# Moving a zero fill from the first mixer to its merge, and four kinds of weight splits from GpSimd to VectorE

## The chip, the cores and the metric

The kernel runs on one core of a Trainium2 chip. The metric is the device time of one execution in microseconds. Engines are named as in the profile: PE (TensorE), DVE (VectorE), ACT (ScalarE), POOL (GpSimd) and SP (SyncE, which here only starts transfers). POOL and ACT start transfers too, each on a queue of its own.

## What is computed

Two layers over 512 tokens of 1024 channels, float32. Each layer has three token mixers on one input, merged by gates, and then a mixture of experts:

```python
def hybrid_mixer(x, w_in, ..., w_up_a, w_up_b, w_up_c, w_out):
    h = x @ w_in                                     # 1024 -> 5632
    u_a, q_b, k_b, v_b, q_c, k_c, v_c, g_c, gate_a, gate_b, gate_c = jnp.split(h, cuts, axis=-1)
    y_a = s5_mixer(u_a, ...)                         # diagonal state space model
    y_b = stick_breaking_attention(q_b, k_b, v_b)
    y_c = chunkwise_retention(q_c, k_c, v_c, g_c, gn_g)
    merged = (jax.nn.sigmoid(gate_a) * (y_a @ w_up_a)
              + jax.nn.sigmoid(gate_b) * (y_b @ w_up_b)
              + jax.nn.sigmoid(gate_c) * (y_c @ w_up_c))
    return merged @ w_out
# then per layer: h = norm(x * ALPHA + mixer(x)); out = norm(h * ALPHA + top-2 of 16 experts(h))
```

## The kernel before

**Products.** Every large product is made of three matmuls of split numbers (`mm3`, L341): a weight `raw` is cast to a high part `wh` on ACT (L337), and the low part `wl = raw - wh` is a subtraction of 128x1024 (L338) on VectorE or on POOL. TensorE then runs high x high (L343), and the two mixed products (L344, L345). `wh` and `wl` have four buffers each in the pool `split`, that is two chunks of two halves.

**Chunks of `w_in`.** Each layer's `w_in` comes in 22 chunks of 256 columns (1 MB), on SP's queue, into two `raw` buffers. Chunk 0 is the S5 input, 1, 2 and 3 are queries, keys and values of the stick-breaking attention, 4 to 9 belong to the retention, and 10 to 21 are the gates, which the merge works off four per branch. Chunks 0, 1, 2 run as `pjf`, chunk 3 as `pjt`. The string `LEND` (L43) says for each chunk which engine makes the low part of each of its halves: 0 is VectorE, 1 is POOL; its last entry holds for all later chunks. A `raw` buffer can be loaded again when both `wl` of the chunk in it are done.

**The attention.** `stick` (L784) runs chunks 1 to 3, then for each unit of heads a score matmul `z`, two sigmoids on ACT (`keep`, `take`, L815 and L816; a table load of ACT goes ahead of the first), a scan and a product on VectorE (L821, L823) and the transposition `pw` on PE (L826).

**S5's power table.** POOL makes parameters of S5 (L578 to L582) and then, in `s5_tables`, the powers `er`, `ei` with help of `Et` in six steps of doubling width, six instructions each (L618 to L623). S5 uses them only after the attention.

**The zero fill.** The experts write into a DRAM tensor `yd` of which 14 blocks of 96 rows by 1024 (the spill rows) must hold zeros. In layer 0, between S5's input and the attention, POOL sets a tile `zr` to zero (L415) and starts two transfers on its own queue (L418), each of 96x14x512 numbers.

**The merge.** For each of 12 gate chunks it loads a piece of an up-projection (`rawu`, cast to `wuh`), runs 48 `pjf` matmuls for the gates and 12 or 24 `up` matmuls. `row_loads` (L955) is a generator: the merge takes one step of it after each chunk, and so spreads the loads of the rows for the later norm (POOL's queue, then POOL's multiplications and additions with `lngb`) over its chunks. `out_proj` follows, with `w_out` loads on SP's queue of which one buffer of each pair lies in the pool `mr`.

**Order.** A scheduler orders the instructions of each engine by priorities when the program is built; each engine then runs its own in that order. `tc.issue_after(x)` keeps what is made under it behind the instruction x. `self.cut` holds the cast and the subtraction of the split that was made last.

Of the kernel before, what the change touches and what calls it, by code (L numbers as in the profile page):

```python
# [9 lines left out]
F32 = mybir.dt.float32  # L10
# [9 lines left out]
P = 128  # L20
T = 512
NT = T // P
D = 1024
# [5 lines left out]
NG = NE - 2  # L29
CAP = 96  # L30
BLOCKS = -(-T // CAP)
SPILL = 2 * T // (CAP + 1) + BLOCKS - 2
# [7 lines left out]
PK = 1  # L40
WGATE = -4
WARM = 16
LEND = ("11", "11", "01", "11", "11", "11", "11", "11", "00")  # L43
BANKS = dict(pj=2, b=2, o=1, z=3)
IN_W = 5632
CHUNK = 8
# [73 lines left out]
class Kernel:  # L120
# [229 lines left out]
    def chunk(self, l, i):  # L350
        if i < len(self.units):
            units, self.units[i] = self.units[i], None
            if units:
                return units
        v, self.early = self.early, None
        if v is None:
            v = self.load_chunk(l, i)
        eng = [self.nc.vector, self.nc.gpsimd]
        hold, self.hold = self.hold, None
        with self.tc.issue_after(hold) if hold else ExitStack():  # L360
            return [self.split_half(v[:, 4 * s:4 * s + 4, :], (4, 256), eng[int(LEND[min(i, len(LEND) - 1)][s])])
                    for s in range(2)]

    def proj_fm(self, l, i, hh):
# [35 lines left out]
    def mixer(self, l, hh, right):  # L400
        with ExitStack() as ms:
            ys = self.slots_of(ms.enter_context(self.pool("ys")), "ys", 8)
            with ExitStack() as rs:
                ev = self.slots_of(rs.enter_context(self.pool("re", "right")), "re", 8)
                with self.pool("s5") as sp:
                    self.mp = sp
                    self.t2 = self.slots_of(sp, "s5", 12)
                    us = self.s5_in(l, hh)
                    self.ahead = AHEAD
                    with self.pool("at", "right") as ap:  # L410
                        self.mp = ap
                        self.t2 = self.slots_of(ap, "at", 14)
                        if l == 0:
                            zr = ys("zr")
                            self.nc.gpsimd.memset(zr, 0.0)  # L415
                            spill = self.y_dram[NG * CAP:, :].rearrange("(i p) d -> p i d", p=CAP)
                            for h in range(2):
                                self.nc.gpsimd.dma_start(spill[:, :, h * T:(h + 1) * T],  # L418
                                                         zr[0:CAP, None, :].to_broadcast([CAP, SPILL, T]))
                        yb = self.stick(l, hh, ys)  # L420
                    self.mp = sp
                    self.t2 = self.slots_of(sp, "s5", 12)
                    ya = self.s5(us, ys)
                rg = ms.enter_context(self.pool("rg"))
                rt = rs.enter_context(self.pool("rt", "right"))
                self.mp = rt
                self.t2 = self.slots_of(rt, "rt", 14)
                yc = self.retention(l, hh, ev, self.slots_of(rg, "yc", 8))
            self.rows = right.enter_context(self.pool("rows", "right"))
            self.mr = right.enter_context(self.pool("mr", "right"))  # L430
            self.t2 = self.slots_of(rg, "mg", 10)
            return self.merge(l, hh, ya, yb, yc)
# [169 lines left out]
    def s5_tables(self):  # L602
        nc = self.nc
        V, G = nc.vector, nc.gpsimd
        w = self.s5w
        En, L, bb, cx = w["En"], w["L"], w["bb"], w["cx"]
        e8 = lambda x: x.rearrange("p (i k) -> p i k", i=8)
        er, ei = e8(self.t2("er")), e8(self.t2("ei"))
        G.memset(er[:, :, 0:1], 1.0)
        G.memset(ei[:, :, 0:1], 0.0)  # L610
        for j in range(6):
            n = 2 ** j
            cr = En[:, 0, :, j:j + 1].to_broadcast([P, 8, n])
            ci = En[:, 1, :, j:j + 1].to_broadcast([P, 8, n])
            a0, b0, a1, b1 = er[:, :, 0:n], ei[:, :, 0:n], er[:, :, n:2 * n], ei[:, :, n:2 * n]
            t01 = self.t2("Et")
            t0, t1 = (e8(t01[:, x * 256:x * 256 + 8 * n]) for x in range(2))
            G.tensor_tensor(a1, a0, cr, OP.mult)  # L618
            G.tensor_tensor(t0, b0, ci, OP.mult)
            G.tensor_tensor(b1, b0, cr, OP.mult)  # L620
            G.tensor_tensor(t1, a0, ci, OP.mult)
            G.tensor_tensor(a1, a1, t0, OP.subtract)
            G.tensor_tensor(b1, b1, t1, OP.add)  # L623
        into = [[], []]
        for h in range(2):
            hs = slice(4 * h, 4 * h + 4)
            f = [4, CHUNK - 1, 16]
            b = [bb[:, r, hs, None, :].to_broadcast([P, *f]) for r in range(2)]
            lam = [L[:, r, hs, 0:CHUNK - 1][:, :, ::-1][:, :, :, None].to_broadcast([P, *f]) for r in range(2)]
            for r in range(2):  # L630
                full = self.t2("vb")
                v = full.rearrange("p (i j c) -> p i j c", i=4, j=CHUNK)
                o = v[:, :, 0:CHUNK - 1]
                x = self.t2("vx")[:, 0:4 * (CHUNK - 1) * 16].rearrange("p (i j c) -> p i j c", i=4, j=CHUNK - 1)
                V.tensor_tensor(o, b[0], lam[r], OP.mult)
                V.tensor_tensor(x, b[1], lam[1 - r], OP.mult)
                V.tensor_tensor(o, o, x, (OP.subtract, OP.add)[r])
                nc.scalar.copy(v[:, :, CHUNK - 1], bb[:, r, hs])
                ps = self.bank("b", "vT")
                for i in range(4):  # L640
                    nc.tensor.transpose(ps[:, i * P:(i + 1) * P], full[:, i * P:(i + 1) * P], self.ident)
                vt = self.t2("V")
                nc.scalar.copy(vt, ps)
                into[r].append(vt)
        tt = self.mp.tile([P, 16 * P], F32, tag="T", name="T", bufs=1)
        t4 = tt.rearrange("p (i g x) -> p i g x", i=8, g=2)
        G.memset(tt, 0.0)
        dI = self.t2("dI")[0:16, 0:256].rearrange("p (i g c) -> p i g c", i=8, g=2)
        d = self.part(w["sm"], "s5_d")[0:16].rearrange("p (i g) -> p i g", g=2)
        V.tensor_tensor(dI, self.ident[0:16, None, None, 0:16].to_broadcast([16, 8, 2, 16]),  # L650
                        d[:, :, :, None].to_broadcast([16, 8, 2, 16]), OP.mult)
        for g in range(2):
            gs = slice(g * 64, g * 64 + 64)
            for h in range(2):
                ps = self.bank("b", "lag")[0:16]
                for i in range(4):
                    for r in range(2):
                        nc.tensor.matmul(ps[:, i * P:(i + 1) * P], bb[gs, r, 4 * h + i],
                                         cx[r][gs, 4 * h + i, 0:CHUNK].rearrange("p m c -> p (m c)"),
                                         start=r == 0, stop=r == 1, skip_group_check=True)  # L660
                hs = slice(4 * h, 4 * h + 4)
                p3 = ps.rearrange("p (i x) -> p i x", i=4)
                nc.scalar.copy(t4[0:16, hs, g, 16:], p3[:, :, 16:])
                V.tensor_tensor(t4[0:16, hs, g, 0:16], p3[:, :, 0:16], dI[:, hs, g], OP.add)
        for j in range(1, CHUNK):
            t3 = tt.rearrange("p (g x) -> p g x", g=16)
            nc.sync.dma_start(t3[j * 16:(j + 1) * 16, :, j * 16:], t3[0:16, :, 0:(CHUNK - j) * 16])
        return er, ei, into, tt
# [286 lines left out]
    def row_loads(self, l):  # L955
        nc = self.nc
# [15 lines left out]
        V.tensor_reduce(self.rc, ps[:, 0:2 * KD * NE].rearrange("p (x k e) -> p x e k", x=2, k=KD), AX.X, OP.add)  # L972
        V.tensor_tensor(self.rc[:, 1], self.rc[:, 1], self.rb, OP.add)
        gb = self.ln_load((self.mr, 2), *(("ln2", l - 1) if l else ("ln0", 0)))
        yield
        for c in range(NT):
            nc.gpsimd.dma_start(self.rt[c], self.h_dram[l][c * P:(c + 1) * P, :])
# [3 lines left out]
                    nc.gpsimd.tensor_tensor(self.rt[c][:, sl], self.rt[c][:, sl], gb[x][:, sl], op)  # L981
            yield
        self.gb = self.ln_load((self.rows, 3), "ln1", l)
        yield

    def out_proj(self, l, mg):
# [581 lines left out]
```

## Time and profile before

| | |
|---|---|
| time, median of 3 runs | 2254.54 us (2254.14 to 2255.88) |
| time of the profiled execution | 2254.74 us |
| its span in the profile | 2253.0 us |
| granted PE clock, mean over the span | 0.977 |
| busy: PE / PE weight load / VectorE | 96% / 72% / 68% |
| busy: ACT / POOL | 55% / 21% |

The span is the time from the first to the last instruction in the trace; the run's own time has 1.74 us around it. Times in the trace are microseconds from the span's start. Layer 0's mixer lies at the start of the span, layer 1's begins at about 1145.

### The profile page before, as it was taken

What the parts mean: (1) busy time and instruction counts of PE and PEld (TensorE: products, weight loads), DVE (VectorE), ACT (ScalarE), POOL (GpSimd) and SP (SyncE); (2) the same over time, 40 slices, a digit from 0 to 9 for tenths busy, and PEclk for the clock granted to TensorE, in tenths of its full rate; (3) what the DMA queues carried; (4) which work ended last, traced back from release to release, by engine and by line L of the source; (5) the groups of instructions that cost most, each with busy time, mean ns of one, the idle gap of its engine ahead of it and who ended that gap; (6) DMA issues with size and microseconds to landing.
All of it is one profiled execution on the core that took longest, in us unless ns stands there. A gap on an engine that the chain in (4) does not pass through costs nothing. (4 is left out here: it accounts for less than half of the span.)

```text
span 2253.0 us, 28020 instructions
## 1 busy us (share of the span) xinstructions
PE 2163.2 (96%) x10500; PEld 1620.2 (72%) x10501; DVE 1540.8 (68%) x1970; ACT 1247.2 (55%) x1580; POOL 479.9 (21%) x509
## 2 busy tenths in 40 slices
PE   7699999999999999999989999999899999999997
PEld 5469678887777777776667887888777777777765
DVE  7144543458988998887853535434799888888877
ACT  3253123336777777776744331233477777777764
POOL 6512051121039930000261302411300000000003
PEclk9799999999999999999999999999999999999999
DMA  5512245327989999997921313352389999999865
GB/s 185 154 29 70 66 150 178 107 94 250 350 297 360 334 361 350 338 366 282 368 94 57 74 56 122 103 187 94 131 310 358 351 356 352 356 351 358 335 258 206
DMA packets 187979, 517.96 MB, mean 230 GB/s; under 512 B 17776, under 2 KB 71664, under 8 KB 187824
## 3 DMA queue, kind: packets, MB, share of 16 engines
q1 hardware_dynamic: 173312, 476.69, 59.1%
q10 hardware_dynamic: 9392, 20.16, 2.6%
q0 software_dynamic: 5120, 19.14, 2.4%
q8 instruction: 85, 1.39, 0.3%
q14 instruction: 70, 0.57, 0.1%
HBM read 490.13 MB, written 22.81 MB: 228 GB/s over the span
## 5 line engine op out<-in xcount | busy, mean ns | idle before, releaser
L338 DVE TENSOR_TENSOR wl<-raw,wh 128x1024 fp32r<-128x1024 f32 x834 | 1018.1, 1240 | 300.9 <-ACT wh L337 286.8
L337 ACT CAST wh<-raw 128x1024 fp32r<-128x1024 f32 x872 | 907.5, 1051 | 463.4 <-PE e L345 196.9
L344 PE MATMUL e<-wl,hx 128*96 128x512 f32 x1024 | 407.2, 398 | 7.1 <-PEq L1453 6.3
L345 PE MATMUL e<-wh,hx 128*96 128x512 f32 x1024 | 404.5, 395 | 0.0
L343 PE MATMUL e<-wh,hx 128*96 128x512 f32 x1024 | 391.3, 394 | 0.3 <-ACT wh L337 0.3
L345 PE MATMUL pjf<-hx,wl 128*128 128x512 f32 x608 | 245.6, 404 | 7.3 <-POOL wl L338 7.3
L343 PE MATMUL pjf<-hx,wh 128*128 128x512 f32 x608 | 246.0, 405 | 4.2 <-DVE v L210 4.2
L344 PE MATMUL pjf<-hx,wh 128*128 128x512 f32 x608 | 245.5, 404 | 0.3 <-DVE hx L211 0.2
L344 PEld LDWEIGHTS e<-wl,hx 128*96 128x96 f32 x1024 | 165.7, 162 | 75.5 <-DVEq L1453 7.2
L1421 POOL DMA_INDIRECT yg<-yd,pos x16 | 28.1, 1753 | 882.2 <-DVE wl L338 585.9
L343 PEld LDWEIGHTS e<-wh,hx 128*96 128x96 f32 x1024 | 165.3, 162 | 67.5 <-ACT wh L337 0.9
L345 PEld LDWEIGHTS e<-wh,hx 128*96 128x96 f32 x1024 | 166.4, 162 | 65.8 <-issue 0.5
L344 PE MATMUL e<-wl,gh 128*96 128x512 f32 x512 | 201.3, 393 | 0.2
L345 PE MATMUL e<-wh,gl 128*96 128x512 f32 x512 | 201.4, 393 | 0.0
L343 PE MATMUL e<-wh,gh 128*96 128x512 f32 x512 | 195.0, 394 | 0.0
L345 PEld LDWEIGHTS pjf<-hx,wl 128*128 128x128 f32 x608 | 116.0, 191 | 35.2 <-POOL wl L338 7.7
L343 PEld LDWEIGHTS pjf<-hx,wh 128*128 128x128 f32 x608 | 116.1, 191 | 32.8 <-DVE v L210 5.5
L344 PEld LDWEIGHTS pjf<-hx,wh 128*128 128x128 f32 x608 | 115.9, 191 | 29.1 <-DVE hx L211 1.4
L821 DVE TENSOR_TENSOR_SCAN left<-keep,cs 128x256 f32<-128x256 f32 (+3 forms) x32 | 27.1, 878 | 142.6 <-ACT keep L815 142.6
L338 POOL TENSOR_TENSOR wl<-raw,wh 128x1024 fp32r<-128x1024 f32 x38 | 96.0, 2537 | 91.8 <-ACT wh L337 91.7
L344 PEld LDWEIGHTS e<-wl,gh 128*96 128x96 f32 x512 | 82.7, 162 | 36.3 <-DVE wl L338 2.2
L343 PEld LDWEIGHTS e<-wh,gh 128*96 128x96 f32 x512 | 82.6, 161 | 35.2
(490 smaller groups left out, 2967.2 us busy)
## 6 DMA issues: line engine op xcount, KB each, us to landing
raw<-in_moe_w_dram SPq DMA_DIRECT2D x384, 1024.0 KB, 5.7
raw<-in_w_in_dram SPq DMA_DIRECT2D x44, 1024.0 KB, 5.2
yd<-y ACTq DMA_DIRECT2D x28, 384.0 KB, 4.8
raw<-in_w_out_dram SPq DMA_DIRECT2D x8, 1024.0 KB, 7.4
yd<-zr POOLq DMA_DIRECT2D x2, 2688.0 KB, 22.2
row<-hd POOLq DMA_DIRECT2D x8, 512.0 KB, 7.3
rawu<-in_w_up_c_dram SPq DMA_DIRECT2D x8, 512.0 KB, 3.5
tab<-in_ct_dram ACTq DMA_DIRECT2D x12, 256.0 KB, 2.8
```

Source lines behind the costliest of these rows:

```text
L337: self.cut = (nc.scalar.copy(hv, v).ins, (eng or nc.vector).tensor_tensor(lv, v, hv.bitcast(F32), OP.subtract).ins)
L338: (eng or nc.vector).tensor_tensor(lv, v, hv.bitcast(F32), OP.subtract).ins)
L343: mm(out, lh, rh, start=start, stop=False)
L344: mm(out, lh, rl, start=False, stop=False)
L345: mm(out, ll, rh, start=False, stop=stop)
L821: V.tensor_tensor_scan(lf[:, 0:n][:, ::-1], keep[:, at:at + n][:, ::-1], self.zero.to_broadcast([P, n]), 1.0, OP.mult, OP.add)
L1421: nc.gpsimd.indirect_dma_start(out=yg[j], out_offset=None, in_=Y[:, :], in_offset=bass.IndirectOffsetOnAxis(ap=r["pos"][:, j, c:c + 1], ax ...
```

## The change

Three edits. The zero fill leaves the place ahead of the attention; in layer 0 `row_loads` now makes a zero tile of 96x1024 in the pool `mr` and starts 14 transfers of 384 KB on ACT's queue, three per step of the generator. `LEND` becomes a table for each layer. And each step of the power table is kept behind `self.cut[1]`.

```diff
-LEND = ("11", "11", "01", "11", "11", "11", "11", "11", "00")
+LEND = (("11", "11", "00", "00", "01", "01", "01", "01", "00"), ("11", "00", "00", "00", "01", "01", "01", "01", "00"))
...
-            return [self.split_half(v[:, 4 * s:4 * s + 4, :], (4, 256), eng[int(LEND[min(i, len(LEND) - 1)][s])])
+            return [self.split_half(v[:, 4 * s:4 * s + 4, :], (4, 256), eng[int(LEND[l][min(i, len(LEND[l]) - 1)][s])])
...
-                        if l == 0:
-                            zr = ys("zr")
-                            self.nc.gpsimd.memset(zr, 0.0)
-                            spill = self.y_dram[NG * CAP:, :].rearrange("(i p) d -> p i d", p=CAP)
-                            for h in range(2):
-                                self.nc.gpsimd.dma_start(spill[:, :, h * T:(h + 1) * T],
-                                                         zr[0:CAP, None, :].to_broadcast([CAP, SPILL, T]))
...
             t01 = self.t2("Et")
+            after = ExitStack()
+            after.enter_context(self.tc.issue_after(self.cut[1]))
             t0, t1 = (e8(t01[:, x * 256:x * 256 + 8 * n]) for x in range(2))
...
             G.tensor_tensor(b1, b1, t1, OP.add)
+            after.close()
...
         gb = self.ln_load((self.mr, 2), *(("ln2", l - 1) if l else ("ln0", 0)))
+        if l == 0:
+            zr = self.mr.tile([P, 2048], F32, tag="raw", name="zr", bufs=2)[0:CAP, 0:D]
+            nc.gpsimd.memset(zr, 0.0)
         yield
...
         self.gb = self.ln_load((self.rows, 3), "ln1", l)
+        yield
+        for i in range(SPILL if l == 0 else 0):
+            nc.scalar.dma_start(self.y_dram[(NG + i) * CAP:(NG + i + 1) * CAP, :], zr)
+            if i % 3 == 2:
+                yield
         yield
```

What this does to the order of the engines, first on POOL in layer 0, where S5's parameters (`s5c`) end and the power table stands. `wl_598` and `wl_602` are the low parts of chunk 3, `wl_1423` is of chunk 4. Before:

```order
L582 TENSOR_SCALAR s5c_97<-s5c_97 128x8x16
L415 MEMSET zr_471 128x512
L338 TENSOR_TENSOR wl_598<-raw_595,wh_597 128x1024 [waits DMAHW3_49,PE_49,Activation_49]
L418 DMA yd_74<-zr_471 96x14x512 [waits Pool_49]
L338 TENSOR_TENSOR wl_602<-raw_595,wh_601 128x1024 [waits PE_49,Activation_49]
L418 DMA yd_74<-zr_471 96x14x512
L622 TENSOR_TENSOR er_982<-er_982,Et_993 128x8x2
L623 TENSOR_TENSOR ei_983<-ei_983,Et_993 128x8x2
L338 TENSOR_TENSOR wl_1423<-raw_1420,wh_1422 128x1024 [waits DMAHW4_49,PE_49,Activation_49]
```

And now, from the same parameter row; the rest of the table stands between, and then the two low parts that POOL keeps here, the second halves of chunks 4 and 5:

```order
L575 TENSOR_SCALAR s5c_97<-s5c_97 128x8x16
L617 TENSOR_TENSOR er_978<-er_978,Et_989 128x8x2 [waits Pool_49]
L618 TENSOR_TENSOR ei_979<-ei_979,Et_989 128x8x2 [waits Pool_49]
...
L617 TENSOR_TENSOR er_978<-er_978,Et_1017 128x8x32 [waits Pool_49]
L618 TENSOR_TENSOR ei_979<-ei_979,Et_1017 128x8x32 [waits Pool_49]
L338 TENSOR_TENSOR wl_1423<-raw_1416,wh_1422 128x1024 [waits DMAHW4_49,PE_49,Activation_49]
L338 TENSOR_TENSOR wl_1503<-raw_1496,wh_1502 128x1024 [waits DMAHW5_49,PE_49,Activation_49]
```

The memset, chunk 3's low parts and the two transfers are gone from this place.

On VectorE in layer 0 the first scan of the attention (`left<-keep`) stood directly behind S5's parameters (`small`). Now these stand there, `wl_594` and `wl_598` being chunk 3's, `wl_1419` and `wl_1499` the first halves of chunks 4 and 5, `vb` and `vx` S5's tables:

```order
L560 TENSOR_TENSOR small_96<-r_364,q_365 128x128
L338 TENSOR_TENSOR wl_594<-raw_591,wh_593 128x1024 [waits DMAHW3_49,PE_49,Activation_49]
L631 TENSOR_TENSOR vb_1024<-small_96,s5c_97 128x4x112 [waits DVE_49]
L338 TENSOR_TENSOR wl_598<-raw_591,wh_597 128x1024 [waits PE_49,Activation_49]
L632 TENSOR_TENSOR vx_1025<-small_96,s5c_97 128x448 [waits DVE_49]
L633 TENSOR_TENSOR vb_1024<-vb_1024,vx_1025 128x4x112 [waits DVE_49]
L338 TENSOR_TENSOR wl_1419<-raw_1416,wh_1418 128x1024 [waits DMAHW4_49,PE_49,Activation_49]
L338 TENSOR_TENSOR wl_1499<-raw_1496,wh_1498 128x1024 [waits DMAHW5_49,Activation_49]
L817 SCALAR_TENSOR_TENSOR left_712<-keep_708,cs_92 128x256 [waits DMAHW1_49,Activation_49]
```

Four subtractions of weights, and the first tables, have come ahead of the scan. In layer 1 both halves of chunk 1 likewise stand right behind the last `hx` of VectorE, then both of chunk 2.

On ACT in layer 0's merge the transfers of the fill (L985) stand between the casts of chunks 12 to 15 (`wh_2374` is chunk 12's second, `wh_2461` and `wh_2465` are chunk 13's) and the gates' activations (`gsg`):

```order
L337 CAST wh_2374<-raw_2368 128x1024 [waits PE_49]
L985 DMA yd_74<-zr_2249 96x1024 [waits Pool_49]
L930 CAST wuh_2433<-rawu_2366 128x512 [waits DMAHW2_49,PE_49]
L939 ACTIVATE gsg_2363<-pjf_2312 128x512 [waits PE_49]
L263 DMA lngb_2703<-in_ln1_g_dram 128x1024 [waits DMAHW1_49]
L263 DMA lngb_2703<-in_ln1_b_dram 128x1024 [waits DMAHW3_49]
L985 DMA yd_74<-zr_2249 96x1024
L985 DMA yd_74<-zr_2249 96x1024 [waits DMAHW5_49]
L337 CAST wh_2461<-raw_2459 128x1024 [waits DMAHW2_49,PE_49]
L939 ACTIVATE gsg_2444<-pjf_2378 128x512 [waits PE_49]
L985 DMA yd_74<-zr_2249 96x1024 [waits DMAHW6_49]
L337 CAST wh_2465<-raw_2459 128x1024 [waits PE_49,Activation_49]
```

Three pieces stand ahead of chunk 13's casts, and one between them; six follow up to chunk 14's first cast, four more up to the last, ahead of chunk 15's. On SP the order is the same as before; there the second `w_out` load of layer 0 now waits for the last piece, since it goes into the buffer of the zeros.

## Rows read from the trace of the kernel before

**Rows 1.** The page, busy time by engine.

```profile
PE 2163.2 (96%) x10500; PEld 1620.2 (72%) x10501; DVE 1540.8 (68%) x1970; ACT 1247.2 (55%) x1580; POOL 479.9 (21%) x509
```

**Rows 2.** Waits of PE: tile, line, releaser; us in total, times, longest.

```profile
PE pw L826 <- DVE take L823: 22.3, 10, 18.5
...
PE pjf L345 <- POOL wl L338: 7.3, 1, 7.3
...
PE pjt L344 <- POOL wl L338: 3.2, 2, 2.4
```

**Rows 3.** Timeline of VectorE: start, us, line, operation, count; idle before and releaser.

```profile
96.95 1.35 DVE L821 TENSOR_TENSOR_SCAN left<-keep,cs 128x256 f32<-128x256 f32 x2 [47.07 <-ACT keep L815]
```

**Rows 4.** Timeline of ACT in layer 0.

```profile
49.05 1.05 ACT L337 CAST wh<-raw 128x1024 fp32r<-128x1024 f32 x1 [1.77 <-PE pjf L344]
...
92.54 1.04 ACT L337 CAST wh<-raw 128x1024 fp32r<-128x1024 f32 x1 [19.39 <-DMA raw<-in_w_in_dram]
...
96.33 0.60 ACT L815 ACTIVATE keep<-z 128x512 f32<-128x512 f32 x1
```

**Rows 5.** Timeline of POOL in layer 0.

```profile
60.60 2.33 POOL L338 TENSOR_TENSOR wl<-raw,wh 128x1024 fp32r<-128x1024 f32 x1
62.89 1.20 POOL L418 DMA_DIRECT2D yd<-zr  x1
64.11 2.37 POOL L338 TENSOR_TENSOR wl<-raw,wh 128x1024 fp32r<-128x1024 f32 x1
```

**Rows 6.** The page, DMA issues: KB each, median us to landing.

```profile
yd<-zr POOLq DMA_DIRECT2D x2, 2688.0 KB, 22.2
```

**Rows 7.** DMA queues from 25 to 110: packets, MB, share of 16 engines.

```profile
q1 hardware_dynamic: 6205, 6.94, 24.5%
q0 software_dynamic: 1376, 5.51, 22.1%
```

**Rows 8.** Timeline of PE: chunk 3, `pw` and the block of 96, both layers.

```profile
60.27 0.28 PE L343 MATMUL pjt<-wh,hx 128*128 128x256 f32 x1
...
100.77 0.69 PE L826 MATMUL pw<-cs,take 128*128 128x128 f32 x2 [18.53 <-DVE take L823]
...
217.66 0.40 PE L343 MATMUL pjf<-hx,wh 128*128 128x512 f32 x1
...
1191.28 0.28 PE L343 MATMUL pjt<-wh,hx 128*128 128x256 f32 x1
...
1208.94 0.44 PE L826 MATMUL pw<-cs,take 128*128 128x128 f32 x2 [0.69 <-DVE take L823]
...
1321.21 0.40 PE L343 MATMUL pjf<-hx,wh 128*128 128x512 f32 x1
```

**Rows 9.** Timeline of POOL in layer 1.

```profile
1147.83 0.47 POOL L618 TENSOR_TENSOR er<-er,s5c 128x8 f32<-128x8 f32 x1
...
1164.01 4.66 POOL L338 TENSOR_TENSOR wl<-raw,wh 128x1024 fp32r<-128x1024 f32 x2
```

**Rows 10.** Window: busy time of PE, PEld, DVE, ACT, POOL; PE clock, DMA share, GB/s.

```profile
1166.00:1172.00 6.00, 5.60 (x13) 4.44 (x14) 0.00 (x0) 0.00 (x0) 5.13 (x7) 0.50 0.38 111
```

**Rows 11.** Timeline of VectorE in layer 1.

```profile
1155.05 1.63 DVE L211 TENSOR_TENSOR hx<-v,hx 128x512 fp32r<-128x512 f32 x2
1156.60 0.84 DVE L635 TENSOR_TENSOR vb<-small,s5c 128x448 f32<-128x448 f32 x1
1157.36 1.43 DVE L338 TENSOR_TENSOR wl<-raw,wh 128x1024 fp32r<-128x1024 f32 x1
```

**Rows 12.** Windows in layer 0's merge, columns as in rows 10.

```profile
290.00:300.00 10.00, 10.00 (x45) 8.11 (x45) 3.81 (x6) 2.17 (x3) 4.89 (x6) 1.00 1.00 358
300.00:310.00 10.00, 10.00 (x44) 8.09 (x43) 3.90 (x2) 3.60 (x5) 10.00 (x8) 1.00 0.35 118
```

**Rows 13.** Timeline of ACT in the merge, chunk 13's first cast.

```profile
305.01 1.05 ACT L337 CAST wh<-raw 128x1024 fp32r<-128x1024 f32 x1 [9.94 <-DMA raw<-in_w_in_dram]
```

**Rows 14.** Timeline of PE in the merge, chunk 13's first matmul.

```profile
310.72 0.40 PE L343 MATMUL pjf<-hx,wh 128*128 128x512 f32 x1
```

**Rows 15.** Timeline of SP's queue in the merge.

```profile
365.79 1.12 SPq L323 DMA_DIRECT2D raw<-in_w_out_dram  x2
```

## The prediction

> **What bounds the kernel now.** I read the page first: TensorE is busy for 2163.2 of the 2253.0 us of the span [rows 1], so an edit to VectorE, GpSimd (POOL) or the DMA queues is worth only what it takes out of TensorE's idle time, or out of its stretches at the lower clock, which count as busy. So the second view is the list of what TensorE waited for [rows 2]: `pw` behind VectorE's `take` with one wait of 18.5 us, the `pjf` matmul of L345 behind a `wl` on POOL with one wait of 7.3, and the `pjt` matmul of L344 behind a `wl` on POOL, 3.2 in two waits. All three lie where the change works.
>
> The long wait is followed back engine by engine. `pw` needs `take`, and VectorE, idle for 47.07 us, did the scan at 96.95 as soon as `keep` was there [rows 3]. ACT made `keep` only at 96.33, since chunk 5's casts stand ahead of it in its queue, and the first had stood for 19.39 us on the load of chunk 5, which landed at about 92.5 [rows 4]. That load goes into the buffer that chunk 3 leaves, free when POOL has done chunk 3's second `wl`, at 64.11 + 2.37 = 66.5. The zero fill had been started on POOL's queue at 62.89, between the two halves [rows 5], and its two DMAs of 2688 KB took 22.2 us to land [rows 6]. So a 1 MB load took 26 us, about as long as the fill. The view of DMA queues for this stretch says why it lost out: POOL's queue (q0) moved 5.51 MB in 1376 packets, 4.0 KB each, the queue of the loads (q1) 6.94 MB in 6205, 1.1 KB each [rows 7].
>
> Two faults in layer 0, then: chunk 3's `wl` are late (casts done by 50.1 [rows 4], subtractions at 60.60 and 64.11 behind S5's parameters and the memset [rows 5]), and chunk 5's load fights the fill. Layer 1 has no fill, and a short form of the first fault: POOL is in the power table from 1147.83, and does chunk 1's two `wl` only from 1164.01 [rows 9]; after the stall TensorE runs at clock 0.50, the lower of its two levels [rows 10].
>
> **Layer 0, step by step.** Removed from here: one memset and two DMA issues on POOL, 5.5 MB of writes. Moved from POOL to VectorE: the `wl` of both halves of chunk 3, of the first halves of chunks 4 to 7, and of the second half of chunk 2. This last one adds one instruction ahead of chunk 3's. VectorE is idle from 96.95 - 47.07 = 49.9 [rows 3], its S5 parameters behind it, and chunk 3's halves stand next in its row; they are cast by 50.1. A `wl` beside a busy POOL took 1.43 us in layer 1 [rows 11]; with chunk 2's ahead and one `vb` of 0.84 [rows 11] between them both are done by 49.9 + 3 x 1.43 + 0.84 = 55.0. TensorE comes to chunk 3 at 60.27 [rows 8]; the two `pjt` waits are gone, and chunk 5's load can start at about 55 and meet no fill, and its cast waits for nothing but the split buffers, which chunk 3's matmuls give back. That is how layer 1 runs this same stretch, so I use layer 1 as the template: from the first `pjt` of chunk 3 to the first matmul of the next 96-matmul block (`sg`) it takes 1321.21 - 1191.28 = 129.93 us, in layer 0 217.66 - 60.27 = 157.39 [rows 8]. The difference, **27.5**, holds the 18.5 wait, the 3.2, and the stretches at lower clock about them.
>
> Two things make layer 0 a little worse than its template. In the template `pw` starts 1208.94 - 1191.28 = 17.7 us into the stretch, 0.69 of them a wait [rows 8]; by the new order TensorE has fewer chunk 4 matmuls ahead of layer 0's `pw` (eight, and the `vT` transposes), which I estimate to leave 1.8 us idle, 1.1 more. And a gap of that size may drop the clock: the one drop for which I have a price is layer 1's, 13 matmuls in 5.60 us at 0.50 [rows 10], where full clock takes 10.00/44 = 0.23 each [rows 12], so 13 x (0.43 - 0.23) = 2.6; at even odds 1.3. From below the two cost 0, from above 3.7. Layer 0: 27.5 - 1.1 - 1.3 = **25.1** (23.8 to 28, the top for a `pjt` that also starts at full clock).
>
> **Layer 1.** Chunk 1's halves go to VectorE, right behind the last `hx`, whose pair ends at 1155.05 + 1.63 = 1156.7 [rows 11]; the first is done at 1156.7 + 1.43 = 1158.1. TensorE asks for it 7.3 us [rows 2] before POOL's 1164.01 + 2.33 [rows 9], at 1159.1. So the wait of 7.25 goes, and with it the 2.6 of lower clock: 9.8, of which I take **9.7**. Margin on the first half is 1.0 us, and the second half is asked for twelve matmuls (2.8 us) later. Beside the table the two could take twice that, 2.9 each; then the first is 0.5 late and the second 0.6, and a clock drop of 2.6 could come on top: 6.5 at the worst, 10 at best. `vb`, `vx` and the rest now lie behind these; VectorE's next scan comes only before `pw` at 1208.94 [rows 8]. What is late next would be the table on POOL; nothing but chunk 4 and 5's second halves stands behind it.
>
> **The table's edge.** `issue_after(self.cut[1])` names the `wl` instruction made last, which is on VectorE after the edit, while all of the table is on POOL. The orders show the table directly behind S5's parameters, both before and now. I cost it at nothing; its cover is that POOL has no other `wl` here but chunk 4's and 5's second halves. In layer 0 the table can go on where POOL now does the memset and the first `wl`, by 60.60 [rows 5], and the whole of it took 1164.01 - 1147.83 = 16.2 in layer 1 [rows 9], so chunk 4's half is done by 60.6 + 16.2 + 2.4 = 79.2 at the latest; TensorE needs it at its thirteenth matmul of the chunk, four behind `pw`, whose start the template puts at 60.27 + 17.7 = 77.9, with z and `pw` work between: about 80.
>
> **The merge.** Added: 14 DMAs of 384 KB on ACT's queue among gate chunks 12 to 14, one memset of 96x1024 on POOL among the row loads. TensorE is busy in 10.00 of 10 here [rows 12], so only a late cast hurts. The trace has no write of this size issued by ACT here; SP's issues of loads took 1.12/2 = 0.56 us [rows 15], POOL's of the fill 1.20 [rows 5]. So 14 issues are 8 to 17 us, spread over about 30, in which ACT is busy for 2.17 to 3.60 of each 10 [rows 12] and has 20 free: both ends hide, and I take 0. The DMA engines are full from 290 to 300 (share 1.00, 358 GB/s) and at 0.35 in the next ten [rows 12]. The first three pieces fall into the full slice: 1.18 MB at 358 GB/s is 3.3 us, at the 250 GB/s (6.5 MB in 26 us) of the old clash 4.7. Chunk 13's load, which now ends at 305.0 [rows 13], would then give its cast at 308.3 to 309.7; TensorE asks for that chunk at 310.72 [rows 14], but the cast (1.05) and a `wl` (2 beside POOL's row additions, an estimate) have to lie before its third matmul at 311.2. So 308.3 + 3.05 = 311.4 costs 0.2, and 309.7 costs 1.6. I take **0.8**; from below 0. The other eleven pieces meet a DMA that is two thirds idle.
>
> **Sum.** 25.1 + 9.7 - 0.8 = 34.0 off the profiled execution's own 2254.74 us (the span and 1.74 around it) gives 2220.7. The median of the runs is 0.2 lower: **2220.5**.
>
> **Rivals.** (A) The sum above: 0.62.
>
> (B) The fill takes its clash along, 0.18. It is 5.5 MB still, and 5.5/0.358 = 15.4 us of all DMA engines. If pieces pass ahead of the loads as they did in layer 0, chunks 13 and 14 each lose the bytes queued ahead of them: six pieces (2.4 MB, 6.6 us) for chunk 14, or a piece that waits on an earlier DMA holds ACT's queue with casts and `gsg` behind it. Against it: 0.35 share in 300:310 [rows 12], 5.7 us of slack on chunk 13 [rows 13, 14]. Price 3 to 7 more: 2223.5 to 2227.5. The Trainium skill bears on it ("DMA: Bandwidth & Descriptors", Queues, rings and completion order): each DMA engine goes round its queues packet by packet. By that rule a fill in 4 KB packets gets some four fifths from a load in 1.1 KB packets whichever queue it is on, and moving it from POOL's queue to ACT's helps nothing in itself. The trace agrees in layer 0, where the load took 26 us and the fill 22.2 [rows 6, 7].
>
> (C) Layer 0's wait only moves, 0.10: the scan stands in VectorE's row behind chunk 5's first half, and that behind ACT's cast and the split buffers; or chunk 4's second half comes behind a table that VectorE's work drew out. For it: the margin of about 1 us of chunk 4's half, worked out above. Against it: layer 1 has the casts ahead of `keep` too and waits 0.69 [rows 8]. Price about 5, with a clock drop up to 9: 2225 to 2230.
>
> (D) The change doesn't do what it says in layer 0, 0.05: another load, not the fill, held chunk 5, and only layer 1's 9.7 and the 3.2 of `pjt` come: 2241.6.
>
> (E) Slower, 0.05. The second pair of `w_out` loads goes into the buffer of the zeros, so SP's queue now waits there for the last piece, with `moe_w`, `w_up_c` and `w_in` loads behind it. Before, it passed at 365.79 [rows 15]. It decides from the point where the last piece lands after that and TensorE runs out of chunks, some 15 us later; to lose the 34 and 4.5 more the last piece would have to land after 365.8 + 15 + 38.5 = 419, though the spare DMA time holds all the pieces by about 335. Price: above 2259.
>
> **The numbers.** The likeliest is 2220.5; A alone spans 2216 to 2224. The range of 8 in 10 takes in B and C and the best case (28 + 10 - 0): 2215 to 2231. About 0.2% (4.5 us) is what a measurement of this kernel can tell from no change. Faster: A to D less a little for mishaps together, 0.93; same 0.03; slower 0.04.
>
> **What would show it.** Right: no wait of `pw` over 3 us, no `pjt` or `pjf` behind a POOL `wl`, chunk 5's cast on ACT before 75, `sg` at 190 to 194, the merge busy 10.00 of 10 in each ten. Wrong: a TensorE wait on an ACT `wh` or VectorE `wl` in the merge (B), `pw` after 80 (C), SP standing at `w_out` (E). The prediction fails most likely by the merge, whose DMA room I know only by slices of ten.

## The result

The change is faster, by a third less than forecast: 2232.61 us median of five runs (2226.74 to 2239.43), against 2254.54 (2253.45 to 2258.44); the ratio is 0.9896, with a 95% interval of 0.987 to 0.9921. Forecast were 2220.5 and a range of 2215 to 2231. The five times lie further apart than those of before; that turns out to be part of the answer.

The profiled run took 2232.61 us with a span of 2230.8, 22.2 below that of before. Cut at the marks of [rows 8] and others of their kind (first `pjt` of chunk 3, first matmul of `sg`, first of `out_proj`), the two profiles compare so, in us:

| stretch | before | after | gain | forecast |
|---|---|---|---|---|
| layer 0, chunk 3 to `sg` | 157.4 | 145.0 | 12.4 | 25.1 |
| layer 0, `sg` to `out_proj` (holds the merge) | 230.0 | 232.8 | -2.8 | -0.8 |
| `out_proj` and experts, to layer 1's first chunk | 698.7 | 697.2 | 1.5 | 0 |
| layer 1, first chunk to chunk 3 | 44.9 | 34.7 | 10.3 | 9.7 |
| layer 1, chunk 3 to `sg` | 129.9 | 129.3 | 0.6 | 0 |

Layer 1's opening came as worked out, and the miss is layer 0. First the waits of TensorE in the changed kernel: tile, line, releaser; us in total, times, longest.

```profile
PE pw L822 <- DVE take L819: 7.5, 8, 4.3
...
PE pjf L345 <- DVE wl L338: 2.1, 1, 2.1
```

The waits behind a `wl` on POOL [rows 2] are gone from the list, and 18.5 of `pw` has become 4.3. The marks on TensorE's timeline:

```profile
60.21 0.28 PE L343 MATMUL pjt<-wh,hx 128*128 128x256 f32 x1
...
80.11 1.12 PE L822 MATMUL pw<-cs,take 128*128 128x128 f32 x4 [4.33 <-DVE take L819]
...
205.19 0.40 PE L343 MATMUL pjf<-hx,wh 128*128 128x512 f32 x1
...
438.02 0.39 PE L343 MATMUL opj<-wh,hx 128*128 128x512 f32 x1
...
1169.89 0.28 PE L343 MATMUL pjt<-wh,hx 128*128 128x256 f32 x1
```

`pw` comes at 80.11, where I had 77.9. ACT, which held it up before [rows 4], now has chunk 5's cast and `keep` in good time:

```profile
70.49 1.05 ACT L337 CAST wh<-raw 128x1024 fp32r<-128x1024 f32 x1 [3.73 <-PE pjt L345]
...
74.77 0.60 ACT L811 ACTIVATE keep<-z 128x512 f32<-128x512 f32 x1
```

On VectorE the scan, which stood idle-ready before [rows 3], starts 3.7 us after `keep` started (3.1 after it ended), behind the first half of chunk 5:

```profile
49.04 1.64 DVE L338 TENSOR_TENSOR wl<-raw,wh 128x1024 fp32r<-128x1024 f32 x1
...
51.56 1.64 DVE L338 TENSOR_TENSOR wl<-raw,wh 128x1024 fp32r<-128x1024 f32 x1
...
71.57 6.98 DVE L338 TENSOR_TENSOR wl<-raw,wh 128x1024 fp32r<-128x1024 f32 x1 [11.72 <-ACT wh L337]
78.47 1.26 DVE L817 TENSOR_TENSOR_SCAN left<-keep,cs 128x256 f32<-128x256 f32 x2
```

Chunk 3's halves took 1.64 each where 1.43 was priced, and were done by 53.2, ahead of the 55.0 priced. But the half of chunk 5 took 6.98 us, more than four times that. What POOL did in those 7 us:

```profile
72.09 0.73 POOL L618 TENSOR_TENSOR ei<-ei,Et 128x256 f32<-128x256 f32 x1
72.77 4.70 POOL L338 TENSOR_TENSOR wl<-raw,wh 128x1024 fp32r<-128x1024 f32 x2
```

POOL, with the end of the table and the second halves of chunks 4 and 5 (the two that `LEND` leaves it), ran without a gap until 77.47, each instruction at its usual length; VectorE's ended 1.1 us later.

The rest of layer 0's miss is in the clock. Windows: the three columns at the end are PE clock, DMA share, GB/s.

```profile
75.00:80.00 5.00, 0.78 (x4) 0.29 (x2) 5.00 (x5) 1.48 (x4) 2.47 (x2) 0.91 0.70 218
80.00:85.00 5.00, 4.89 (x15) 2.78 (x16) 2.08 (x5) 0.77 (x2) 0.10 (x1) 0.50 0.60 202
...
115.00:120.00 5.00, 5.00 (x23) 2.95 (x22) 2.16 (x5) 2.12 (x5) 0.13 (x2) 0.50 0.02 3
```

After a slice with 0.78 us of work in 5, TensorE is granted 0.50 (1.2 GHz). It happens a second time from 113 to 127, with no wait of `pw` over 0.8 us ahead of it.

In the merge the one wait, 2.1 us, is chunk 13's. The load was late: the cast came 11.4 us after chunk 12's first gate matmul at 284.71, where before it was 8.3 (296.72 to 305.01 [rows 13]). That still left 2.7 us before TensorE asked. Then it looks much like the first wait: VectorE's two `wl` of that chunk took 5.41 us, the first of them 4.28, while POOL did its row additions. Before, the two took 3.99 beside the same additions.

```profile
296.06 1.05 ACT L337 CAST wh<-raw 128x1024 fp32r<-128x1024 f32 x1 [12.98 <-DMA raw<-in_w_in_dram]
```

```profile
297.14 5.41 DVE L338 TENSOR_TENSOR wl<-raw,wh 128x1024 fp32r<-128x1024 f32 x2 [11.47 <-ACT wh L337]
```

```profile
287.81 12.52 POOL L980 TENSOR_TENSOR row<-row,lngb 128x512 f32<-128x512 f32 x10
```

### The profile page after: what moved, and what is told of

The parts are those of the page before. It is cut to its first block, busy times and chain, and to the rows that moved or that the text cites. A ratio compares the mean times of both kernels' runs of the same rounds, so it can differ in the third digit from the quotient of the medians.

```text
span 2230.8 us, 28031 instructions
## 1 busy us (share of the span) xinstructions
PE 2161.2 (97%) x10498; PEld 1617.5 (73%) x10501; DVE 1554.7 (70%) x1986; ACT 1246.3 (56%) x1580; POOL 437.3 (20%) x491
## 5 line engine op out<-in xcount | busy, mean ns | idle before, releaser
L338 DVE TENSOR_TENSOR wl<-raw,wh 128x1024 fp32r<-128x1024 f32 x850 | 1046.1, 1250 | 342.2 <-ACT wh L337 328.6
L345 PEld LDWEIGHTS e<-wh,gl 128*96 128x96 f32 x512 | 82.5, 161 | 34.3
L1212 PE MATMUL gx<-A,hi 128*128 128x288 f32 (+1 forms) x640 | 97.3, 296 | 0.0
```

The lines of the kernel that those rows point to most:

```text
L338: (eng or nc.vector).tensor_tensor(lv, v, hv.bitcast(F32), OP.subtract).ins)
L345: mm(out, ll, rh, start=False, stop=stop)
L1212: nc.tensor.matmul(ps[s], rows[c][:, k * P:(k + 1) * P], A[:, c].rearrange("p e s -> p (e s)"), start=c == 0, stop=c == NT - 1)
```

## The experiments

Three theories stood after this. **1**: VectorE gets no turn while POOL runs instructions that read SBUF back to back; what POOL kept in layer 0 costs the scan, and then the clock. **2**: the clock falls because this attention is thin in matmuls, whatever VectorE does. **3**: part of the miss comes and goes between executions. And of the change's parts (the fill, the subtractions by `LEND`, and the edge, which keeps the table behind the last split) it was open which does what. "Mark" below is the stretch from chunk 3 to `sg` in layer 0: 157.4 before, 145.0 with the change.

**All of chunks 4 and 5 on VectorE (e1).**

```diff
-LEND = (("11", "11", "00", "00", "01", "01", "01", "01", "00"), (...))
+LEND = (("11", "11", "00", "00", "00", "00", "01", "01", "00"), (...))
```

> The changed kernel, but in layer 0 the second halves of chunks 4 and 5 also go to VectorE, so that POOL has no subtraction of weights near the attention's first scan. Theory 1 (the first half of chunk 5 on VectorE took 6.98 us because POOL's table and its two subtractions ran at the same time, and the scan stood behind it): each wl takes under 2 us, the first wait of pw falls from 4.3 to under 1.5 us, the stretch at the lower clock from 80 to 88 is gone, and the time falls by the wait and that stretch, 3.3 + 3.7 = 7, to about 2226. Theory 2 (the clock falls because this attention has few matmuls in flight, whatever VectorE does): the long wl is gone, but the lower clock stays at two places and the time stays within 3 of 2232.

2220.99 us median of five (2218.03 to 2231.3), ratio 0.9852 (0.9832 to 0.9873). VectorE's timeline, then TensorE's:

```profile
71.56 4.49 DVE L338 TENSOR_TENSOR wl<-raw,wh 128x1024 fp32r<-128x1024 f32 x2 [8.93 <-ACT wh L337]
75.98 1.26 DVE L817 TENSOR_TENSOR_SCAN left<-keep,cs 128x256 f32<-128x256 f32 x2
```

```profile
77.61 0.66 PE L822 MATMUL pw<-cs,take 128*128 128x128 f32 x3 [1.14 <-DVE take L819]
```

Two `wl` now take less than one did, though the first of them, beside the table's last steps, took 3.36, where I had expected under 2. `pw` comes 2.5 us sooner, within my 77.6 to 77.9, and the mark is 133.5, a gain of 23.9 where the prediction had 25.1. The lower clock after it shrank to part of one slice (0.69 from 80 to 85), and the second stretch was not there. In e7 below, whose layer 0 is that of e1, and in e6 this lower clock is gone too, and the mark is 132.1 and 132.2: a gain of 25.3 and 25.2. The wait's share is theory 1's; the time fell further than it said.

**Is it POOL's reading (e5 and e6)?** Both kernels are e1 with work added on POOL directly behind layer 0's table, on a tile that is used up by then:

```diff
+                for _ in range(4):
+                    G.tensor_tensor(t01, t01, t01, OP.add)
```

in e5, and in e6

```diff
+                for _ in range(9):
+                    G.memset(t01, 0.0)
```

> e1_c45_vector with four additions of 128x512 on POOL, directly behind layer 0's power table; nothing reads their result, they stand in for the two subtractions that e1 took away from there, and take about as long, 5 us. Theory 1 (a VectorE instruction with two SBUF inputs gets no turn while POOL runs instructions that read SBUF back to back): VectorE's two wl of chunk 5, 4.49 us together in e1 from 71.56, last until POOL is through at about 78.5 and 2.5 more, the scan starts at about 80.5 instead of 75.98, and the first pw at about 82. Rival (the wl was long because of its own data, chunk 5's load or cast): as in e1, 4.5 us, pw at 77.6.

> As e5_pool_adds, but with nine memsets of 128x512 (0.52 us each, 4.7 in all) in place of the additions: POOL is as busy, but reads no SBUF. Theory 1 as the Trainium skill words it (SBUF: the lock holds against a GpSimd operation that reads SBUF): VectorE's two wl end as in e1 once the table is through, within 4.5 to 5 us, scan at about 76, pw at 77.6. Rival (any POOL instruction keeps VectorE out): as e5, scan at about 80, pw at 82.

With the additions, VectorE and POOL:

```profile
71.79 5.30 DVE L339 TENSOR_TENSOR wl<-raw,wh 128x1024 fp32r<-128x1024 f32 x2 [8.95 <-ACT wh L338]
77.02 2.90 DVE L823 TENSOR_TENSOR_SCAN left<-keep,cs 128x256 f32<-128x256 f32 x2
79.84 1.53 DVE L825 TENSOR_TENSOR take<-take,left 128x256 f32<-128x256 f32 x2
```

```profile
74.11 6.64 POOL L625 TENSOR_TENSOR Et<-Et 128x512 f32<-128x512 f32 x4
```

With the memsets:

```profile
71.56 4.48 DVE L339 TENSOR_TENSOR wl<-raw,wh 128x1024 fp32r<-128x1024 f32 x2 [8.93 <-ACT wh L338]
75.97 1.26 DVE L823 TENSOR_TENSOR_SCAN left<-keep,cs 128x256 f32<-128x256 f32 x2
```

```profile
73.88 5.18 POOL L625 MEMSET Et<- 128x512 f32 x9
```

Nine memsets beside them leave VectorE's instructions as they were in e1 to a hundredth; four additions stretch all of them, and `pw` goes to 81.09. So it is what the additions do and the memsets don't, reading SBUF above all, and not POOL's being busy. But the additions did not shut VectorE out as my numbers said: the two `wl` grew by 0.8, the scans took 2.90 instead of 1.26, the products 1.53 instead of 0.72. Each addition depends on the one ahead, the two `wl` of the change do not; that the gaps between dependent additions let VectorE in is a reading of this, not tested. (The times of these single runs, 2231.6 and 2227.8, hold lower clock elsewhere: from 102 to 116 the one, from 1194 to 1208 the other.)

Nor is it a rule that VectorE is the one kept out, as theory 1 has it. In layer 1 of the changed kernel VectorE's four `wl` of chunks 1 and 2 ran beside the table and took 1.40 each. There it was the table's instructions that grew: this one, of 128x128, took 1.44, where in layer 0 it took 0.45.

```profile
1145.48 5.60 DVE L338 TENSOR_TENSOR wl<-raw,wh 128x1024 fp32r<-128x1024 f32 x4
```

```profile
1147.16 1.44 POOL L617 TENSOR_TENSOR er<-er,Et 128x128 f32<-128x128 f32 x1
```

What decides which of the two engines waits, these runs don't settle.

**The change once more (e9).**

> The changed kernel itself once more, for the five times from 2226.7 to 2239.4. If the stretch at the lower clock from 113 to 128 in its profile comes and goes from one execution to the next (theory 3), the profile shows the same first wait of pw of 4.3 and the same lower clock behind it, but the second stretch may be gone or elsewhere, and then layer 0's mark sg is near 199 and the time near 2226. Rival (the second stretch belongs to this order of instructions): it is there again at 113, sg at 205, time within 2 of 2232.6.

2228.56 us median of six (2224.49 to 2238.19), ratio 0.9895 (0.9878 to 0.9912). The profile has the same 4.4 us wait and the clock drop behind it, and where the second stretch was:

```profile
115.00:120.00 5.00, 5.00 (x30) 2.89 (x28) 2.41 (x6) 2.80 (x7) 0.13 (x2) 1.00 0.00 0
```

Full clock. The mark is 136.4, 8.5 less than in the first profile of the same kernel, and the run took 2224.49. By the starts of ACT's instructions, the same in both, 6.1 of the 8.5 lie between 110 and 128. The rest lies about the first drop, 0.50 from 79 to 89 in the first profile and from 81 to 88 here, and about a third stretch, from 164 to 178 there and from 160 to 170 here. Theory 3 holds for the second stretch, and theory 2 falls as it stands: the same instructions in the same order ran at either level. Whether the drop needs a thin attention stays open.

**The fill elsewhere (e2, the edit in part).** In the attention, where the DMA engines have next to nothing to do from 85 to 130 (a share of 0.02 or less in windows of 5 us):

```diff
+                if self.fill and h2 == 0 and unit[0] in ((1, 0), (1, 3)):
+                    with self.tc.issue_after(last):
+                        h = unit[0][1] // 3
+                        nc.gpsimd.dma_start(self.fill[0][:, :, h * T:(h + 1) * T],
+                                            self.fill[1][0:CAP, None, :].to_broadcast([CAP, SPILL, T]))
```

> The changed kernel, but the fill is issued on POOL's queue as two transfers behind the fourth and fifth unit of layer 0's attention, where no load is under way, instead of 14 pieces on ACT's queue in the merge. Theory 1 (the fill holds up chunk 13's load, and with it one wl beside POOL's row additions): the TensorE wait of 2.1 us in the merge goes, from the gates' first matmul of layer 0 to out_proj it takes 230.0 again instead of 232.8, and the time is about 2.8 lower, 2230. Rival (the merge's wait is one of VectorE and POOL alone): the merge still takes over 232, no gain.

2225.03 us median of five (2223.67 to 2235.29), ratio 0.9859 (0.9844 to 0.9874). No TensorE wait is left in the merge, and from chunk 12's first gate matmul to `out_proj` it takes 150.95 us, as before the change, where the changed kernel takes 153.31. So the fill's price in the merge is 2.4 by these two profiles. It is more in others with the fill there: in e9's the same stretch takes 154.76, 3.8 more than before, as the same wait of 2.1 has a stretch at 0.50 from 293 to 296 behind it; e3, e5, e6 and e7 have 154.8 to 154.9, e1 has 153.3. The mark from `sg` that I had named is no good here: it is 233.5, since the clock was lower from 228 to 235, ahead of the merge.

**The fill where it was (e4, against the changed kernel, in part).**

```diff
+                            for h in range(2):
+                                self.nc.gpsimd.dma_start(spill[:, :, h * T:(h + 1) * T],
+                                                         zr[0:CAP, None, :].to_broadcast([CAP, SPILL, T]))
...
-            nc.scalar.dma_start(self.y_dram[(NG + i) * CAP:(NG + i + 1) * CAP, :], zr)
```

> The fill stays where it was, on POOL's queue ahead of the attention; LEND by layers and the edge as in the change. Theory 1 (the fill's fight with chunk 5's load is the greater part of layer 0's loss): layer 1 gains its 10; in layer 0 chunk 3 runs without a wait, but chunk 5's load meets the fill and pw waits some 8 to 15 us. Time 2236 to 2244. Rival (only the late subtractions matter): within 3 of the changed kernel, 2230 to 2236.

2225.77 us median of four (2223.9 to 2227.37), ratio 0.9868 (0.9853 to 0.9883). Both my theories are wrong here. POOL started the fill at 63.17, and ACT's timeline has chunk 5's cast at the same moment as the changed kernel, waiting for TensorE and for no load:

```profile
70.49 1.05 ACT L337 CAST wh<-raw 128x1024 fp32r<-128x1024 f32 x1 [3.73 <-PE pjt L345]
```

With chunk 3's `wl` done at 52.3, its `raw` buffer is free some ten us ahead of the fill, and no clash with that load is left to avoid. `pw` waits 6.0, but for VectorE, whose `wl` beside POOL took 8.44, and the mark is 138.7, 2.3 more than e9's. From `sg` to `out_proj` it takes 230.1 again.

**Fill moved, subtractions left on POOL (e3).** `LEND` as before, the edge kept:

> The fill moved and the table kept behind the last split, with LEND as before in both layers, so all subtractions of chunks 3 to 5 are on POOL. Theory 1 (without the fill, chunk 5's load is in time, and the rest is what VectorE gives): layer 0 keeps part of the gain, chunk 3's low parts come about 0.5 us earlier than before and cost about 2.5 us, and the table runs ahead of chunk 4's, which are then 4 us late; layer 1 gains less than 1, or loses, as its table now stands behind chunk 3. Time 2240 to 2247. Rival (all of layer 0's gain comes from VectorE): over 2250.

2247.58 us median of ten (2236.95 to 2253.56), ratio 0.9965 (0.9953 to 0.9977). Without chunk 3 on VectorE the move of the fill seems to count: the mark is 144.4 in its profile (13.0 less than before). But that profile is of the fastest of the ten, 10.6 below their median, and against the edge alone (e11, below), which differs by nothing but the fill, the intervals of the two ratios just overlap. POOL's four `wl` now hold up the scan itself, on VectorE's timeline:

```profile
78.93 7.01 DVE L817 TENSOR_TENSOR_SCAN left<-keep,cs 128x256 f32<-128x256 f32 x2 [25.70 <-ACT keep L811]
```

**The edge alone (e11)**, in the kernel before:

> The kernel before with nothing but the edge: the table is kept behind the last split, all fill and LEND as before. Theory 1: layer 1's table goes behind chunk 3's subtractions, so the wait of 7.25 there goes without any work for VectorE, 7 to 9 us; in layer 0 the fill still holds chunk 5's load (pw waits some 18), so 2246 to 2249. Rival (the edge does nothing of itself, as I costed it): within 2 of before.

2251.11 us median of ten (2248.19 to 2261.52), ratio 0.9986 (0.9972 to 1.0). That can hardly be told from no change. In the profile layer 1's opening falls from 44.9 to 39.2 us, and its 7.25 wait is gone with no work for VectorE; layer 0's mark is 3.4 longer in its profile, with a wait of 18.0 and lower clock in most slices from 80 to 120.

**Layer 1's splits as before (e7)**, on top of e1:

> e1_c45_vector with layer 1's splits as they were before the change (layer 0 as in e1). My term for layer 1 says 9.7: the wait of pjf behind POOL is back at about 7.2 us, with a stretch at the lower clock, and the time is 9.7 above e1, 2230 to 2231. Rival (layer 1's gain is taken back by its own later waits): within 4 of e1.

2231.77 us median of four (2225.77 to 2233.41), ratio 0.9879 (0.9861 to 0.9898). I had overlooked that the edge stays in force here. POOL's timeline has the table behind chunk 3's halves, no longer ahead of chunk 1's [rows 9]:

```profile
1154.88 0.23 POOL L613 TENSOR_TENSOR er<-er,s5c 128x8 f32<-128x8 f32 x1
```

The wait that I had named is not back, so that the time came near my 2230 to 2231 is luck. The opening takes 39.2, as in e11, so in layer 1 the edge alone gives 5.7 of the 10.3 (7.3 in e3, whose profile has no lower clock there). In the change itself it moves nothing: the instruction that it names is on VectorE there, and the table starts at 1136.71, ahead of that at 1159.69. So the 10.3 are VectorE's. Of the 12.2 us that this profile takes more than e1's, 8.2 lie in layer 1's attention, with lower clock from 1210 to 1224.

**Together.** Two ways to have both the free POOL and the free merge, the first with the fill where it was (e8), the second with the fill in the attention (e10):

> e1_c45_vector, but with the zero fill where it was before the change, on POOL's queue ahead of the attention. Theory 1 (with chunk 3's subtractions on VectorE, chunk 5's load is through before the fill starts, so the move of the fill brings nothing and costs the merge 2.8): about 2.8 below e1, 2218. Rival (the fill still meets a load, chunk 5's or 6's): pw waits over 2 us, or the retention's first chunk waits for a cast, and the time is above e1's 2221.

2221.51 us median of five (2220.78 to 2222.7), ratio 0.9844 (0.9831 to 0.9858). The merge is 230.0 again, but the fill's memset and issues push the table's end to 75.2, over chunk 5's `wl`, the first of which took 4.78: `pw` at 80.01, mark 136.5. What the merge gets back the attention loses.

> e1_c45_vector with the fill as in e2, on POOL's queue behind the fourth and fifth unit of the attention. The two single effects added: e1's attention (pw at 77.6, sg at 193) and e2's merge (no wait on wl, under 231 from sg to out_proj), so e1's 2221.0 less 2.3 to 2.8, about 2218.5. Rival (the two DMA issues on POOL, 1.2 and 0.95 us, hold up VectorE's next scans, or the clock falls elsewhere): no better than e1.

2219.77 us median of five (2218.02 to 2230.01), ratio 0.9853 (0.9836 to 0.987). Merge 229.9, mark 134.4. e1, e8 and e10 can't be told apart by their times, nor e1 from e2 and e4; the intervals of e1, e8 and e10 lie below that of the change's second measurement (0.9878 to 0.9912).

## Why the prediction was wrong

- **Layer 0's 25.1**: the step that failed is "two things make layer 0 a little worse than its template", 1.1 and 1.3. A third stood in the orders that I had shown: chunk 5's half on VectorE ahead of the scan, and POOL's table and two `wl` behind it at the same time. In layer 0 I had priced a `wl` beside a busy POOL for chunk 3 only, by one row of 1.43, and then took layer 1 as the template, where the table is through long before. It measured 6.98, the first wait of `pw` 4.3 where 1.8 was put, and the scan came 2.5 later than in e1. With POOL's two `wl` gone the mark falls from 136.4 (the change, e9) to 133.5 in e1 and 132.1 in e7, so their price is 2.9 to 4.3, clock included. That was rival (C)'s place, at somewhat less than its price of about 5, with another cause than the one I gave it. Its sign came too: `pw` after 80.
- **The clock**, priced at 2.6 with even odds: one drop did follow the longer wait. But the larger loss is 8.5 us that one profile of the changed kernel has and the other hasn't, 6.1 of it in the second stretch of lower clock, from 113 to 127. The eleven times of the changed kernel run from 2224.5 to 2239.4, those of the kernel before, 46 in all its measurements, from 2253.5 to 2262.9. I had no such term, since before has none in this place. Why the clock falls there in one execution and not in the other, the runs don't say. That the first median, 2232.61, lies above my range and the second, 2228.56, inside it is this chance; the step above failed in both profiles.
- **The merge's 0.8** was 2.4 (2.8 with what came ahead of it), and 3.8 in e9's profile, where lower clock follows the wait, which I had not priced. The place was right, chunk 13, and the load was 3.1 late, close to the 3.3 to 4.7 that I had put. The cast came at 296.06, 2.7 before TensorE asked. The term of the wrong size is the `wl` beside POOL's row additions: 2 by my estimate, 4.28 for the first here, done 1.1 us after the additions were; with 2 it would have been just in time. The two had taken 1.74 and 2.32 before. Why the first is shut out here and not there is not shown. The ACT issues cost nothing, as bounded.
- **The fill and chunk 5's load**: I had counted "two faults". They were one. The load met the fill only because chunk 3's `wl` were late (e4). With them on VectorE the move only takes a memset and two issues off POOL, ahead of the table's end: 2.3 of the mark (e4 against e9) and 3.1 (e8 against e1), about what it costs the merge. With all subtractions on POOL it may pay more (e3).
- **Layer 1's 9.7** measured 10.3, and its cause as told. **The edge** at nothing: right for this change, whose order is the same with and without it, but wrong as a statement on the edge, which alone takes 5.7 out of layer 1 (e11).
- **Rivals**: (B) half true, by 1.6 more than my term, or 3.0 with the lower clock; (D) and (E) were not seen: SP passed `w_out` at 356.18, 9.6 earlier than before [rows 15], with no wait.
- The sum: 12.7 less in layer 0 (8.5 that e9 does not lose, 2.9 POOL, and 1.2 by which e1 stays behind, which e6 and e7 don't have), 2.0 less from there to `out_proj`, 2.9 more elsewhere, nearly all of it after that: 34.0 became 22.2 by the profiles. Of the 2.9, 1.5 lie in the experts, where nothing was changed, and seem to go with the clock: before it was 0.83 and 0.50 in the two slices of 5 us from 1060, with the change 0.66 in the one from 1055. The edge alone, on the kernel before, has 1.00 there and the shorter time too (696.8), and e2, with 0.76 and 0.55 from 1045, the longer (698.8).

## What to carry to other kernels

Moving work from GpSimd to VectorE is priced by what GpSimd still does at that moment: look at both queues side by side, and at what stands behind the moved instruction. Before a transfer is moved away from a clash, ask what made it start late; freeing the buffer sooner can end the clash with the transfer where it is. And where times spread by several us, compare two profiles of the same kernel before giving a difference a cause.

## What the runs showed of the hardware

A VectorE subtraction of 128x1024 with both inputs in SBUF took 1.2 us with POOL idle, 1.64 beside short POOL instructions, and 6.98, 7.48 (e2) and 8.44 (e4) beside a POOL that ran `tensor_tensor` back to back, whose own instructions kept their length (2.35 for a `wl`). A scan pair went from 1.26 to 7.01 in the same way (e3). Beside memsets nothing changed (e6). The Trainium skill ("SBUF — State Buffer", SBUF: two separate sides) has this as an exclusive lock on a port pair, which a VectorE instruction with two SBUF inputs contends for only against a GpSimd operation that reads SBUF, whoever comes first keeping it for the whole instruction. The runs agree on what collides. They add that POOL instructions in a row can keep VectorE out over their boundaries too: the half of chunk 5 waited through the end of the table and two `wl`. But they need not: in layer 1 four `wl` on VectorE beside the table took 1.40 each and the table's instructions grew, and in the merge of before two `wl` beside POOL's row additions took 3.99.

A stretch of 14 us at the lower clock was there in one execution of the changed kernel and not in another. Layer 1's attention, which e1, e2 and e6 leave alone, took 129.3, 136.3 and 136.3 us.
